# Low parts of the weights in the heads' stage: on VectorE instead of GpSimd, and two projection steps later

## The chip, the cores and the metric

The kernel runs on one core of a Trainium2 chip. The core's engines work side by side, each through its own queue of instructions in a fixed order: TensorE (PE in the profile, its weight loads PEld), VectorE (DVE), ScalarE (ACT), GpSimd (POOL) and SyncE (SP), whose queue issues most DMAs. The metric is the device time of one execution in microseconds; lower is better.

## The reference, cut to what matters

One layer of a hybrid encoder on 528 prompt positions and 128 sample positions, in fp32. One projection `w_in` feeds eight heads of gated delta rule and a state space model (S5); both go through one output projection, a layer norm and a gated feed-forward network.

```python
proj = h @ w_in                                   # (656 x 2048) @ (2048 x 5136)
qkv_pre, z, a_logit, b_logit, u = split(proj)
qkv = silu(conv4(qkv_pre)); q, k = l2_normalize(q), l2_normalize(k)
...                                               # per head, over blocks of positions:
w = w_val_c - k_cd_c @ s                          # s: the 128 x 128 state
o = q_dec_c @ s + qk_c @ w
s = s * g_tot_c + k_dec_c.T @ w
...
o = o * rsqrt(mean(o * o) + eps) * dn_norm_w * silu(z)
y5 = s5_ssm(u); y5 = gelu(y5); y5 = y5 * sigmoid(y5 @ s5_w_glu + s5_b_glu)
x1 = layer_norm(alpha * h + concat(o, y5) @ w_out)
y = layer_norm(alpha * x1 + (silu(x1 @ w_gate) * (x1 @ w_up)) @ w_down)
```

## The kernel before

A product of fp32 matrices is made of three products in the faster fp32r format. Each operand is split in a high part and a low part, and a tile of output sums high × high, low × high and high × low. The activations are split once (`hh`, `hl`); the weights are split as they come in, in units of 128 × 1024.

The life of one weight unit goes through four places. `push` notes a load, a DMA into a tile `raw` of which there are two. `halves` makes `whi` (a copy to fp32r on ScalarE, L160) and the low part `wlo` (`raw` minus `whi`, L161); there are three buffers of each. `advance` calls both ahead of need, and `unit` hands the oldest unit out. `project` uses it: a projection has two units, each of two halves of eight steps of three matmuls, `pj<-hh,whi`, `pj<-hl,whi` and `pj<-hh,wlo` (L498 to L500). When the second half of a unit begins, `project` calls `advance(2)`, which makes the parts of the unit two further on; so a weight made in one unit is used one whole unit later.

The engine of the low parts comes from `self.lows`, an endless list. It holds VectorE in the S5 stage and from the GLU on; `heads_phase` sets it to GpSimd (L700).

The heads' stage runs from 340 to 935 us. `heads_phase` gives `drive` a row of generators (`fill`: the projections of q, k, v of six heads, of z of eight, then the GLU) and a list of jobs with step numbers. A projection yields after every six matmuls; such a stretch is a projection step, and after each one `drive` advances the jobs that are due. Head h begins 47 steps after head h − 1, with three jobs: `delta_prep` (transposes, the decay `dt`, the blocks `gt` and `qk`, the prepared rows `vc` of L847, the inverse of a triangular block by `inv16`, and an inverse root in steps named `nrm`), `delta_double` (the inverse, doubled up) and `delta_scan` (the chain over the blocks). In the scan each block goes TensorE (`ps_seq<-st,kq`, L992, L993), VectorE (`rhs`, L995, and the sum `vc` of L978), TensorE (L1001), ScalarE (`x`), TensorE (L1006), VectorE (the new state `st`, L1011), and again; the sample positions go beside it (`srhs` L1034, `xm` L1045, `sb` L1047 and L1056). At its end come an inverse root (steps named `rms`), the scaled rows `vc` (L956) and their transposes on TensorE (L393).

A context `behind` adds an order that no data asks for: an instruction in it comes after a given one, on whatever engine. `drive` puts each job's step behind the last matmul so far, and `project` puts the parts of a unit there. A scheduler makes each engine's order from the program, the dependencies and these orders.

GpSimd does in this stage, per head, the scaling of `gt` (L857, three instructions), of `sb` (L1047), the masked block `gm` (L889), a few small copies, and the low parts.

Of the kernel before, what the change touches and what calls it, by code (L numbers as in the profile page):

```python
# [11 lines left out]
F32 = mybir.dt.float32  # L12
# [82 lines left out]
class Builder:  # L95
    def __init__(self, tc, io, stop=None):
        self.tc, self.nc, self.io, self.stop = tc, tc.nc, io, stop
        self.booted = None
        self.lows = cycle([self.nc.vector])
        self.units = []  # L100
        self.loaded = []
        self.issued = []
        self.quads = []
        self.raws = []
        self.later = deque()
# [45 lines left out]
    def halves(self, val, n):  # L151
        nc = self.nc
        w = val.shape[1]
        hi = self.wp.tile([P, 1024], F32R, name="whi", tag="whi", bufs=3)[:, :w]
        lo = self.wp.tile([P, 1024], F32R, name="wlo", tag="wlo", bufs=3)[:, :w]
        if self.booted is None:
            nc.vector.tensor_copy(hi, val)
            nc.gpsimd.tensor_sub(lo, val, hi.bitcast(F32))
        else:
            nc.scalar.activation(hi, val, AF.Copy)  # L160
            next(self.lows).tensor_sub(lo, val, hi.bitcast(F32))  # L161
        return hi.rearrange("p (k n) -> p k n", n=n), lo.rearrange("p (k n) -> p k n", n=n)

    def advance(self, ahead):

        while self.units and len(self.issued) < ahead:
            if not self.loaded:
                self.loaded.append(self.units[0][0]())
            self.issued.append(self.units.pop(0)[1](self.loaded.pop(0)))
        if self.units and not self.loaded:  # L170
            self.loaded.append(self.units[0][0]())

    def unit(self, ahead=2):
        self.advance(1 + ahead)
        return self.issued.pop(0)


# [185 lines left out]
    def drive(self, fill, jobs):  # L363


        jobs = [[x, n, lo, hi, 0] for x, n, lo, hi in jobs]

        def advance(at):
            for job in jobs:
                x, n, lo, hi, _ = job  # L370
                while job[4] <= n and job[4] * (hi - lo) < n * (at - lo):
                    job[4] += 1
                    with self.behind(self.last.ins):
                        if next(x, self) is self:
                            job[4] = n + 1
            if self.later:
                with self.behind(self.last.ins):
                    if next(self.later[0], self) is self:
                        self.later.popleft()

        at = 0
        for at, _ in enumerate(chain(*fill), 1):
            advance(at)
        while self.later or any(job[4] <= job[1] for job in jobs):
            at += 1
            advance(at)
# [307 lines left out]
    def heads_phase(self):  # L694
        self.head = {}

        self.gm16, self.pp16 = (self.dl.tile([96, 5, 96], F32, name=x) for x in ("gm16", "pp16"))
        for x in (self.gm16, self.pp16):
            self.nc.gpsimd.memset(x, 0.0)
        self.lows = cycle([self.nc.gpsimd])  # L700
        self.left = 2 * (3 * (H - PRE) + H)
        fill = [self.qkv(h) for h in range(PRE, H)] + [self.project_z(i) for i in range(H)]
        fill += [self.glu_start()] + [self.glu(m) for m in range(8)]
        jobs = []
        for h in range(H):
            at = PERIOD * h
            jobs.append((self.delta_prep(h), 23, at, at + 23))
            jobs.append((self.delta_double(h), 8, at + 30, at + 54))
            jobs.append((self.delta_scan(h), 35, at + 54, at + 2 * PERIOD + 2))
        jobs.append((self.gelu(), 8, 290, 390))  # L710
        jobs.append((self.glu_load(), 1, 396, 397))
        jobs.append((self.glu_split(), 4, 408, 422))
        self.drive(fill, jobs)
        self.nc.sync.dma_start(self.io["o_conv"], self.co)

    def qkv(self, h):
# [832 lines left out]
    def w_out(self):  # L1549
        tc, nc, io = self.tc, self.nc, self.io  # L1550
        v, a, g = nc.vector, nc.scalar, nc.gpsimd
        with tc.tile_pool(name="acc", bufs=1, side="right", reuse_waits="tile") as ap:
# [83 lines left out]
            def step(nm, i):  # L1636
                x, y = halves(i)
                if nm == "T1":
                    o = x[:, 0:8]
                    v.tensor_sub(o, y[:, 0:8], o)  # L1640
                elif nm == "T2":
                    o = x[:, 0:8]
                    v.tensor_sub(o, y[:, 8:16], o)
                elif nm == "T3":
                    o = y[:, 0:8]
                    g.tensor_sub(o, y[:, 8:16], o)
                elif nm == "B22":
                    o = y[:, 8:16]
                elif nm == "T4":
                    o = x[:, 8:16]  # L1650
                    g.tensor_sub(o, o, x[:, 0:8])
                    nc.sync.dma_start(self.scr_f.rearrange("k p n -> p k n")[:, :, 64 * i : 64 * i + 64], o)
                    return
                put(nm, o, 64 * i, 64)
# [399 lines left out]
```

## Time and profile before

| | |
|---|---|
| time, median of 3 runs | 2956.07 us (2953.01 to 2960.33) |
| the profiled execution | 2958.67 us, its span 2956.8 us |
| TensorE busy over the span | 2817.0 us, 95% |
| VectorE, ScalarE, GpSimd busy | 2248.6, 1174.9, 469.4 us (76, 40, 16%) |
| the chain that ended last, by engine | TensorE 71%, VectorE 15%, DMA 4%, issue 3%, ScalarE 2%, GpSimd 1% |
| mean granted TensorE clock over the span | 0.985 of full speed |

The span is what the trace covers; the time is a little longer. The shares are means over stages, so the heads' stage is read by itself, in a window. Of an engine's wait the profile names the instruction whose end released it. The durations in the timelines are from start to end of an instruction: one that stands still while it runs shows as a long one.

### The profile page before, as it was taken

The numbers are of one execution on the slowest core, as the hardware profiler recorded it, in microseconds if no ns is written. First come the engines' busy times: TensorE is split into PE (matmuls) and PEld (weight loads), VectorE is DVE, ScalarE is ACT, GpSimd is POOL, SyncE is SP. The second block draws the span as 40 slices with busy tenths as digits, with TensorE's granted clock in tenths as the row PEclk, the third lists the DMA queues.
The fourth block names the chain that finished last, engine by engine and source line by source line (L and its number), as shares of the span: only waits on it lengthen the run. The fifth ranks groups of instructions, "written<-read, shape, count | busy, mean of one in ns | idle before, by whom it ended". The sixth has DMA issues, their size and how long they took to land.

```text
span 2956.8 us, 47411 instructions
## 1 busy us (share of the span) xinstructions
PE 2817.0 (95%) x18707; PEld 2694.2 (91%) x18707; DVE 2248.6 (76%) x3715; ACT 1174.9 (40%) x2141; POOL 469.4 (16%) x371
## 2 busy tenths in 40 slices
PE   6999999999899999889999999999999999999996
PEld 5999988888889878689999999999999999999995
DVE  9899776666655744897878787878888667778788
ACT  3555334444434513643434343434343343323234
POOL 3122333233221300430000000000000021111114
PEclk9999999999999999999999999999999999999998
DMA  4333333433446634553434443444444645553553
GB/s 157 102 107 102 109 95 89 98 88 89 126 126 207 218 102 131 152 155 117 148 117 148 117 149 117 148 117 144 122 148 119 238 139 202 203 183 111 188 179 128
DMA packets 477983, 409.14 MB, mean 138 GB/s; under 512 B 50708, under 2 KB 424644, under 8 KB 473392
## 3 DMA queue, kind: packets, MB, share of 16 engines
q1 hardware_dynamic: 475960, 403.01, 44.6%
q8 instruction: 147, 2.41, 0.4%
q10 hardware_dynamic: 1800, 3.11, 0.3%
q14 instruction: 76, 0.62, 0.1%
HBM read 319.80 MB, written 86.26 MB: 137 GB/s over the span
## 4 chain that ended last, share of the span: by engine, by line
PE 71%; DVE 15%; DMA 4%; issue 3%; ACT 2%; POOL 1%; SPq 0%; DVEq 0%; ACTq 0%; POOLq 0%
PE pb_m L1474 14%; PE pb_m L1476 14%; PE pb_m L1475 14%; PE pd L1476 5%; PE pd L1474 5%; PE pd L1475 5%; PE pj L498 3%; PE pj L500 3%; PE pj L499 3%; DVE wlo L161 2%; ACT whi L160 1%; DVE pr L782 1%; DMA raw<-in_w_out 1%; PE ps_prep L393 1%; DVE z L1353 1%
## 5 line engine op out<-in xcount | busy, mean ns | idle before, releaser
L160 ACT ACTIVATE whi<-raw 128x1024 fp32r<-128x1024 f32 x408 | 431.4, 1057 | 600.8 <-PE pb_m L1476 148.7
L161 DVE TENSOR_TENSOR wlo<-raw,whi 128x1024 fp32r<-128x1024 f32 x330 | 424.7, 1287 | 166.4 <-ACT whi L160 165.7
L161 POOL TENSOR_TENSOR wlo<-raw,whi 128x1024 fp32r<-128x1024 f32 x78 | 190.4, 2442 | 1624.6 <-ACT whi L160 1608.7
L498 PE MATMUL pj<-hh,whi 128*128 128x328 f32 (+1 forms) x1248 | 424.9, 340 | 0.0
L500 PE MATMUL pj<-hh,wlo 128*128 128x328 f32 (+1 forms) x1248 | 395.6, 317 | 0.0
L499 PE MATMUL pj<-hl,whi 128*128 128x328 f32 (+1 forms) x1248 | 394.9, 316 | 0.0
L160 ACT ACTIVATE whi<-rq 128x1024 fp32r<-128x1024 f32 x190 | 201.5, 1061 | 376.1 <-PE pb_m L1475 257.8
L1474 PE MATMUL pd<-hp,whi 128*128 128x320 f32 x960 | 297.9, 310 | 8.4 <-ACT whi L160 8.4
L1476 PE MATMUL pd<-hp,wlo 128*128 128x320 f32 x960 | 298.0, 311 | 1.8 <-POOL wlo L161 1.3
L1475 PE MATMUL pd<-hp,whi 128*128 128x320 f32 x960 | 297.6, 310 | 0.0
L498 PEld LDWEIGHTS pj<-hh,whi 128*128 128x128 f32 x1248 | 238.2, 191 | 17.5 <-issue 14.7
L499 PEld LDWEIGHTS pj<-hl,whi 128*128 128x128 f32 x1248 | 238.4, 191 | 1.0 <-issue 0.8
L500 PEld LDWEIGHTS pj<-hh,wlo 128*128 128x128 f32 x1248 | 237.4, 190 | 0.5 <-issue 0.2
L161 DVE TENSOR_TENSOR wlo<-rq,whi 128x1024 fp32r<-128x1024 f32 x176 | 224.2, 1274 | 15.6 <-ACT whi L160 14.6
L193 DVE TENSOR_TENSOR raw<-rq 128x1024 f32<-128x1024 f32 x128 | 158.6, 1239 | 60.7 <-DMA rq<-in_ffn_w_gate 31.2
L1800 DVE TENSOR_TENSOR s<-pb_m,s 128x320 f32<-128x320 f32 x308 | 149.8, 487 | 69.8 <-PE pb_m L1476 67.8
L1905 DVE TENSOR_TENSOR acf<-acf,pd 128x640 f32<-128x640 f32 x184 | 146.8, 816 | 70.4 <-PE pd L1476 69.6
L1474 PEld LDWEIGHTS pd<-hp,whi 128*128 128x128 f32 x960 | 181.5, 189 | 9.5 <-ACT whi L160 9.5
L1476 PEld LDWEIGHTS pd<-hp,wlo 128*128 128x128 f32 x960 | 181.6, 189 | 3.0 <-POOL wlo L161 2.0
L1475 PEld LDWEIGHTS pd<-hp,whi 128*128 128x128 f32 x960 | 181.5, 189 | 0.0
L1811 ACT ACTIVATE hh<-hq 128x560 fp32r<-128x560 f32 (+1 forms) x88 | 57.6, 654 | 158.3 <-DMA scr_h<-hh 74.7
L1475 PE MATMUL pb_m<-T2l,whi 128*128 128x320 f32 x352 | 109.5, 311 | 3.4 <-DVE T2l L1629 3.4
(585 smaller groups left out, 7657.9 us busy)
## 6 DMA issues: line engine op xcount, KB each, us to landing
rq<-in_ffn_w_gate SPq DMA_DIRECT2D x88, 512.0 KB
rq<-in_ffn_w_up SPq DMA_DIRECT2D x88, 512.0 KB
raw<-in_w_in SPq DMA_DIRECT2D x80, 512.0 KB
rq<-in_ffn_w_down SPq DMA_DIRECT2D x80, 512.0 KB
raw<-in_w_out SPq DMA_DIRECT2D x48, 512.0 KB
hp<-scr_h SPq DMA_DIRECT2D x18, 1280.0 KB
scr_h<-hh SPq DMA_DIRECT2D x80, 280.0 KB
scr_h<-hq SPq DMA_DIRECT2D x20, 1120.0 KB
```

The lines of the kernel that those rows point to most:

```text
L160: nc.scalar.activation(hi, val, AF.Copy)
L161: next(self.lows).tensor_sub(lo, val, hi.bitcast(F32))
L193: self.nc.vector.tensor_tensor(o, x, y, op=op)
L498: nc.tensor.matmul(o, whi[:, k], self.h_hi[u][:, k, s], start=(kk == 0), stop=False)
L499: nc.tensor.matmul(o, whi[:, k], self.h_lo[u][:, k, s], start=False, stop=False)
L500: self.last = nc.tensor.matmul(o, wlo[:, k], self.h_hi[u][:, k, s], start=False, stop=(kk == KT - 1))
L1474: mm(out, sh, mh, start=first, stop=False)
L1475: mm(out, sh, ml, start=False, stop=False)
L1476: self.last = mm(out, sl, mh, start=False, stop=last)
L1800: v.tensor_tensor(t, x, y, op=ALU.add)
L1811: a.activation(h, x, AF.Copy)
L1905: v.tensor_tensor(x, x, ps, op=ALU.subtract if o[0] == "-" else ALU.add)
```

## The change

`halves` no longer issues the low part in the heads' stage. It notes it in a list `due` with a count of two. After every projection step `drive` counts down and issues what has come to zero, behind the last matmul, on the engine that `self.lows` gives. `heads_phase` no longer sets that to GpSimd, so it is VectorE. `advance` and `unit` issue all that is still due. After `drive` the list is off again; the units of the GLU inside `drive` are noted in it too.

```diff
--- before.py
+++ after.py
@@ -96,6 +96,7 @@
     def __init__(self, tc, io, stop=None):
         self.tc, self.nc, self.io, self.stop = tc, tc.nc, io, stop
         self.booted = None
+        self.late_lows, self.due = False, []
         self.lows = cycle([self.nc.vector])
         self.units = []
         self.loaded = []
@@ -158,11 +159,23 @@
             nc.gpsimd.tensor_sub(lo, val, hi.bitcast(F32))
         else:
             nc.scalar.activation(hi, val, AF.Copy)
+            if self.late_lows:
+                self.due.append([2, lo, val, hi])
+            else:
+                next(self.lows).tensor_sub(lo, val, hi.bitcast(F32))
+        return hi.rearrange("p (k n) -> p k n", n=n), lo.rearrange("p (k n) -> p k n", n=n)
+
+    def low_parts(self, steps=None):
+
+        for x in self.due:
+            x[0] -= 1
+        while self.due and (steps is None or self.due[0][0] <= 0):
+            _, lo, val, hi = self.due.pop(0)
             next(self.lows).tensor_sub(lo, val, hi.bitcast(F32))
-        return hi.rearrange("p (k n) -> p k n", n=n), lo.rearrange("p (k n) -> p k n", n=n)
 
     def advance(self, ahead):
 
+        self.low_parts()
         while self.units and len(self.issued) < ahead:
             if not self.loaded:
                 self.loaded.append(self.units[0][0]())
@@ -172,6 +185,7 @@
 
     def unit(self, ahead=2):
         self.advance(1 + ahead)
+        self.low_parts()
         return self.issued.pop(0)
 
 
@@ -366,6 +380,8 @@
         jobs = [[x, n, lo, hi, 0] for x, n, lo, hi in jobs]
 
         def advance(at):
+            with self.behind(self.last.ins):
+                self.low_parts(1)
             for job in jobs:
                 x, n, lo, hi, _ = job
                 while job[4] <= n and job[4] * (hi - lo) < n * (at - lo):
@@ -697,7 +713,7 @@
         self.gm16, self.pp16 = (self.dl.tile([96, 5, 96], F32, name=x) for x in ("gm16", "pp16"))
         for x in (self.gm16, self.pp16):
             self.nc.gpsimd.memset(x, 0.0)
-        self.lows = cycle([self.nc.gpsimd])
+        self.late_lows = True
         self.left = 2 * (3 * (H - PRE) + H)
         fill = [self.qkv(h) for h in range(PRE, H)] + [self.project_z(i) for i in range(H)]
         fill += [self.glu_start()] + [self.glu(m) for m in range(8)]
@@ -711,6 +727,7 @@
         jobs.append((self.glu_load(), 1, 396, 397))
         jobs.append((self.glu_split(), 4, 408, 422))
         self.drive(fill, jobs)
+        self.late_lows = False
         self.nc.sync.dma_start(self.io["o_conv"], self.co)
 
     def qkv(self, h):
```

The order on GpSimd, beside the fourth head's scan, before (names are out<-in; `co`, `xp` are the convolution's small copies):

```order
L624 COPY xp<-scT 128x8x3
L161 TENSOR_TENSOR wlo<-raw,whi 128x1024
L857 TENSOR_TENSOR gt<-gt,fc 112x3x112
L857 TENSOR_TENSOR gt<-gt,fc 96x2x96
L857 TENSOR_TENSOR gt<-gt,fc 128x128
L161 TENSOR_TENSOR wlo<-raw,whi 128x1024
L1047 TENSOR_TENSOR sb<-sb,ee 128x1024
L635 COPY co<-xp 128x3
L636 COPY co<-xp 128x24
L161 TENSOR_TENSOR wlo<-raw,whi 128x1024
L624 COPY xp<-scT 128x8x3
L889 TENSOR_TENSOR gm_4018<-gt,consts 96x15x16
```

The same place after the change (line numbers are those of the changed program, up to 17 higher):

```order
L640 COPY xp<-scT 128x8x3
L874 TENSOR_TENSOR gt<-gt,fc 112x3x112
L874 TENSOR_TENSOR gt<-gt,fc 96x2x96
L874 TENSOR_TENSOR gt<-gt,fc 128x128
L1064 TENSOR_TENSOR sb<-sb,ee 128x1024
L651 COPY co<-xp 128x3
L652 COPY co<-xp 128x24
L640 COPY xp<-scT 128x8x3
L906 TENSOR_TENSOR gm_4018<-gt,consts 96x15x16
```

The low parts are gone from GpSimd, the rest stands in the same order; all 52 of the stage are gone so.

The order on VectorE in the fourth head's scan, from a step of the inverse's copying (`pr`) to the first sums of the block, before (`nrm_*` is the inverse root of the next head):

```order
L782 TENSOR_TENSOR pr<-pr,ti 41x512
L118 TENSOR_TENSOR nrm_t<-nrm_t,ss 128x6
L1011 SCALAR_TENSOR_TENSOR st<-st,ee,ps_seq 128x128
L789 TENSOR_REDUCE ti<-pr 41x8x8
L119 SCALAR_TENSOR_TENSOR nrm_y<-nrm_t,nrm_y 128x6
L642 SCALAR_TENSOR_TENSOR yc<-xp,cwc,yc 128x680
L794 COPY ti<-ti 41x16x16
L117 SCALAR_TENSOR_TENSOR nrm_t<-nrm_y 128x6
L995 SCALAR_TENSOR_TENSOR rhs<-ps_seq,fc,vc 96x128
L118 TENSOR_TENSOR nrm_t<-nrm_t,ss 128x6
L978 TENSOR_TENSOR vc<-o_7405,ps_seq 112x128
```

And after:

```order
L799 TENSOR_TENSOR pr<-pr,ti 41x512
L119 TENSOR_TENSOR nrm_t<-nrm_t,ss 128x6
L1028 SCALAR_TENSOR_TENSOR st<-st,ee,ps_seq 128x128
L806 TENSOR_REDUCE ti<-pr 41x8x8
L120 SCALAR_TENSOR_TENSOR nrm_y<-nrm_t,nrm_y 128x6
L658 SCALAR_TENSOR_TENSOR yc<-xp,cwc,yc 128x680
L811 COPY ti<-ti 41x16x16
L118 SCALAR_TENSOR_TENSOR nrm_t<-nrm_y 128x6
L174 TENSOR_TENSOR wlo<-raw,whi 128x1024
L119 TENSOR_TENSOR nrm_t<-nrm_t,ss 128x6
L1012 SCALAR_TENSOR_TENSOR rhs<-ps_seq,fc,vc 96x128
L120 SCALAR_TENSOR_TENSOR nrm_y<-nrm_t,nrm_y 128x6
```

One low part has come in, behind the state `st` and ahead of the next `rhs`.

The order on VectorE at the end of the first head's scan, up to the start of the root `rms` (L927 waits for the doubled inverse), before:

```order
L623 MEMSET xp 128x3
L649 SCALAR_TENSOR_TENSOR kq<-kq,yc 128x528
L650 SCALAR_TENSOR_TENSOR kq<-kq,yc 128x128
L1011 SCALAR_TENSOR_TENSOR st<-st,ee,ps_seq 128x128
L978 TENSOR_TENSOR vc<-o_5225,ps_seq 96x128
L927 TENSOR_SCALAR rt<-ps_inv 32x5x32
L949 TENSOR_SCALAR ms<-ms 128x6
```

And after:

```order
L639 MEMSET xp 128x3
L174 TENSOR_TENSOR wlo<-raw,whi 128x1024
L665 SCALAR_TENSOR_TENSOR kq<-kq,yc 128x528
L916 TENSOR_TENSOR rt<-rt,ps_inv 96x5x3x16
L666 SCALAR_TENSOR_TENSOR kq<-kq,yc 128x128
L1028 SCALAR_TENSOR_TENSOR st<-st,ee,ps_seq 128x128
L995 TENSOR_TENSOR vc<-o_5225,ps_seq 96x128
L944 TENSOR_SCALAR rt<-ps_inv 32x5x32
L966 TENSOR_SCALAR ms<-ms 128x6
```

A low part has come in ahead of the last state `st` of the head, and a small instruction of the inverse (`rt`, L916) has moved in between; the root `rms` itself follows unchanged.

## Rows read from the trace of the kernel before

**Rows 1.** The page, part 1: busy us (share of the span) and instructions of each engine.

```profile
PE 2817.0 (95%) x18707; PEld 2694.2 (91%) x18707; DVE 2248.6 (76%) x3715; ACT 1174.9 (40%) x2141; POOL 469.4 (16%) x371
```

**Rows 2.** Windows, heads' stage: us, busy PE, PEld, DVE, ACT, POOL, PEclk, DMA share, GB/s.

```profile
340.00:935.00 595.00, 562.08 (x4067) 518.30 (x4067) 381.16 (x1044) 239.81 (x771) 174.56 (x150) 0.98 0.42 111
```

**Rows 3.** TensorE's waits, 340 to 935 us: us in total, times, longest.

```profile
PE ps_seq L992 <- DVE st L1011: 12.4, 6, 3.2
PE ps_seq L1040 <- issue: 4.5, 2, 3.4
PE ps_seq L393 <- DVE vc L956: 4.3, 4, 2.3
PE ps_seq L1054 <- DVE vc L978: 2.9, 3, 2.3
PE ps_prep L393 <- DVE vc L847: 1.9, 3, 1.2
PE ps_prep L832 <- DVE vc L847: 1.9, 1, 1.9
PE ps_inv L892 <- DMA tt<-scr_r: 1.9, 1, 1.9
PE ps_seq L1031 <- DMA sb<-in_state_delta: 0.8, 1, 0.8
```

**Rows 4.** Instructions of line 161, 340 to 935 us: duration ns min/median/max, first and last.

```profile
L161 POOL TENSOR_TENSOR wlo<-raw,whi x52: 2357/2390/2828, 347.8 to 926.0; 128x1024 fp32r<-128x1024 f32 x52
```

**Rows 5.** The same line, 60 to 340 us.

```profile
L161 DVE TENSOR_TENSOR wlo<-raw,whi x28: 1198/1217/1589, 69.8 to 338.9; 128x1024 fp32r<-128x1024 f32 x28
```

**Rows 6.** Timeline of three engines near 640 us (start us, us), and line 864's instructions.

```profile
635.98 2.39 POOL L161 TENSOR_TENSOR wlo<-raw,whi 128x1024 fp32r<-128x1024 f32 x1 [4.37 <-ACT whi L160]
635.96 2.42 DVE L864 TENSOR_SCALAR own<-consts,ee 128x2 f32<-128x2 f32 x1
643.51 0.46 PE L992 MATMUL ps_seq<-st,kq 128*96 128x128 f32 x2 [2.23 <-DVE st L1011]
L864 DVE TENSOR_SCALAR own<-consts,ee x8: 212/216/2423, 373.3 to 848.1; 128x2 f32<-128x2 f32 x8
```

**Rows 7.** Timeline, GpSimd and VectorE near 777 us, and a like instruction.

```profile
776.48 2.76 POOL L161 TENSOR_TENSOR wlo<-raw,whi 128x1024 fp32r<-128x1024 f32 x1 [10.84 <-ACT whi L160]
776.95 3.16 DVE L782 TENSOR_TENSOR pr<-pr,ti 41x512 f32<-41x512 f32 x1
642.13 1.00 DVE L782 TENSOR_TENSOR pr<-pr,ti 41x512 f32<-41x512 f32 x1
```

**Rows 8.** Timeline, VectorE and GpSimd near 464 us.

```profile
463.17 0.31 DVE L927 TENSOR_SCALAR rt<-ps_inv 32x160 f32<-32x160 f32 x1 [1.95 <-PE ps_inv L922]
464.62 2.42 POOL L161 TENSOR_TENSOR wlo<-raw,whi 128x1024 fp32r<-128x1024 f32 x1 [3.16 <-ACT whi L160]
464.81 2.25 DVE L118 TENSOR_TENSOR rms_t<-rms_t,ms 128x6 f32<-128x6 f32 x1
```

**Rows 9.** Timeline, VectorE: first and last of the 29 held instructions.

```profile
368.94 2.27 DVE L642 SCALAR_TENSOR_TENSOR yc<-xp,cwc,yc 128x680 f32<-128x680 f32 x1
927.06 1.99 DVE L1430 TENSOR_TENSOR hl<-ge,hh 128x640 fp32r<-128x640 f32 x1
```

**Rows 10.** Waits of SP's DMA queue, 340 to 935 us: us in total, times, longest.

```profile
SPq L146 <- POOL wlo L161: 28.1, 14, 5.5
```

**Rows 11.** Timeline, VectorE and TensorE just after rows 6.

```profile
645.17 0.33 DVE L995 SCALAR_TENSOR_TENSOR rhs<-ps_seq,fc,vc 96x128 f32<-96x128 f32 x1
646.25 0.46 PE L1001 MATMUL ps_seq<-rhs,rt 96*96 96x128 f32 x2 [0.19 <-DVE vc L978]
```

**Rows 12.** Windows of 4 us, columns as in rows 2.

```profile
782.00:786.00 4.00, 3.71 (x16) 3.71 (x17) 2.85 (x13) 1.17 (x5) 0.00 (x0) 0.57 0.46 81
```

**Rows 13.** Timeline, GpSimd and VectorE near 756 us.

```profile
755.74 1.57 POOL L857 TENSOR_TENSOR gt<-gt,fc 112x336 f32<-112x336 f32 x3 [4.94 <-DVE fc L854]
755.90 3.61 DVE L1397 TENSOR_SCALAR gt__8801<-gt__8801 128x640 f32<-128x640 f32 x1 [0.25 <-ACT gt__8801 L1396]
```

## The prediction

> **What bounds the kernel now.** First the page: TensorE is busy 95% of the span [rows 1], so the time falls only where TensorE stands still or runs slowly, or where matmuls go away; the change takes away none. Then the table by stage. The change is confined to the heads' stage, 340 to 935 us: there TensorE is busy 562 of 595 us, VectorE 381 and GpSimd 175, at a mean granted clock of 0.98 [rows 2]. So 33 us of standing still and some slow running are all that can be won here. Third, TensorE's waits in that stage by what ended them [rows 3]: 12.4 us for the state `st` of the scan, 4.3 for the normalised rows `vc` (L956), 4.5 for `srhs` (named "issue"), 2.9 for `vc` (L978), twice 1.9 for the prepared `vc` (L847), 1.9 for a DMA of the inverse. Nearly all of them end with a VectorE instruction; none ends with a low part of a weight. VectorE is 64% busy, so over the stage it isn't the bound: these waits come from single late instructions.
>
> **Why those instructions are late.** Each of the 52 low parts runs 2.39 us on GpSimd [rows 4]; 52 × 2.39 = 124 of GpSimd's 175 us. In the stage before this one the same instruction, on VectorE, takes 1.22 us [rows 5]. Now look at the two engines side by side. GpSimd starts a low part at 635.98 and takes 2.39; VectorE's `own`, two columns wide, starts at 635.96 and takes 2.42 us where its kind takes 0.21 to 0.22, ending with it; TensorE then waits 2.23 us for `st` [rows 6]. The same at 776.48: a `pr` takes 3.16 us, against 1.00 for the like one at 642.13 [rows 7], and the longest wait for `st`, 3.2 us, follows. And at 464.62: one small step of the inverse root takes 2.25 us [rows 8], and TensorE waits for the `vc` that ends the chain. I compared each VectorE instruction under a low part with the short ones of its form: 29 of the 52 cases run over 0.6 us too long, 52 us in all; the first took 2.27 us, the last 1.99 [rows 9]. The other 23 hold next to nothing, VectorE being idle or in an instruction that isn't held.
>
> The Trainium skill has the rule for it (SBUF — State Buffer, § SBUF: two separate sides): VectorE and GpSimd share a pair of ports that is an exclusive lock, held for the whole instruction, and who starts first blocks the other. Held rows that end with the low part agree with it. By the same rule a moved low part, which reads two SBUF operands, can itself be held by what stays on GpSimd; that would add an estimated 3 us of VectorE time and change the sum by less than its rounding.
>
> **The change, part by part.** *Removed:* 52 instructions on GpSimd, 124 us, and with them 52 us of held VectorE time. *Added:* 52 low parts on VectorE, 52 × 1.22 = 63 us. VectorE's net load rises by about 11 us, to 66% of the stage. *Moved:* each low part now enters two projection steps later. That is 12 matmuls; by 562 us for 4067 matmuls one takes 0.138 us [rows 2], so 1.7 us. It ends at about 1.7 − 2.39 + 1.22 = 0.5 us later than today. A weight made in one unit is used a whole unit later, 48 matmuls or 6.6 us, and no wait of today ends with a low part [rows 3], so I cost the delay at nothing; if VectorE's queue stood over 6 us behind, that cover would be gone and each case cost what exceeds it. The low part's end also frees the raw tile, and SP's queue stands still for that: 28.1 us in 14 waits, up to 5.5, and every DMA behind the waiting one with it [rows 10]. 0.5 us more in each of 14 is 7 us of SP's time; TensorE's waits that end with a DMA are the inverse's 1.9 and one of 0.8 for a state [rows 3], so at most 2 × 0.5 = 1 us of it can reach TensorE today. I take 0, and leave the 1 us to the range. The remaining units of the GLU get the two steps too; their low parts are on VectorE already.
>
> What the waits give back, one by one:
> - `st`, 12.4 us in six waits. At 643.51 the hold is 2.42 − 0.21 = 2.2 us. By the order of after, the low part now stands behind `st` and ahead of `rhs`. `rhs` ends at 645.50 and TensorE waits again at 646.25, 0.19 us [rows 11]: no slack there. So VectorE runs 2.2 us earlier up to `st`, only 2.2 − 1.2 = 1.0 earlier after it, and TensorE gains about 1.0 and not 2.2. In five of the six the low part is ahead of `st` or of the next `rhs`, in one behind both. The ends are 6 × 1.0 = 6 and the full 12.4; I take 1.4 each, 8.4, nearer to the case worked out.
> - `vc` L956, 4.3 us in four waits. Here the low part stands well ahead of the chain, before an instruction for which VectorE sat idle 1.95 us [rows 8], and the next one right behind the last `vc`. So most of it goes: 3.4; ends 1.5 (where the low part fills the place of the hold) and 4.3.
> - `vc` L978, 2.9: two waits follow a held instruction; 1.2, ends 0 and 2.9.
> - `vc` L847, 3.8 in the two rows: one of the waits, 1.9, follows a late DMA and stays; 1.0 of the rest, ends 0 and 1.9.
> - the inverse's DMA, 1.9: the chain ahead of it was held three times, and TensorE's instruction that waits moves some four projection groups later by the order; 1.0, ends 0 and 1.9.
>
> Together 8.4 + 3.4 + 1.2 + 1.0 + 1.0 = 15.0 us, ends 7.5 and 23.4.
>
> *The clock.* After the long wait at 782 the granted clock is 0.57 for 4 us [rows 12], that is mostly the lower level, 1.2 GHz; there are six such stretches, each after a wait of 1.9 us or more. A mean of 0.98 over 595 us costs about 12 us (6 to 18 by its rounding). Where the waits shrink, some of these stretches go: I take 5 us, ends 0 and 10.
>
> *Against it:* a low part that lands in front of an instruction that TensorE waits for, where today no hold was. The nearest row is the low part's own 1.22 us [rows 5]; 23 of the 52 replace a hold of nearly nothing. I take 2 us for two such places, ends 0 and 32 (below).
>
> *What stays:* GpSimd keeps `gt` (1.57 us per head) and, right behind it, `sb`; the two hold a GELU instruction on VectorE for 3.61 us, and the 3.4 us wait for `srhs` follows [rows 13], which I leave in full.
>
> Sum: 15.0 + 5 − 2 = 18 us off the profiled 2958.67, some 2941; that run lies 2.6 over the median 2956.07, so the forecast is **2938**.
>
> **Rivals.** *1. The hold is only exchanged.* In every case the 1.2 us sit in the same backlog that the 2.2 us sat in, each wait shrinks by the low end (7.5 in all), the stretches at half clock stay, and new waits cost 2: 2956.1 − 5.5 = 2950.6, no change. For it speaks the case at 643.51; against it that in the chain of `vc` VectorE has an idle 1.95 us for it. *2. VectorE becomes the bound (slower).* Low parts enter at fixed steps of the projection; where VectorE is in a backlog already, as around 636 to 643, each pushes `st`, `rhs` or `srhs` back. If half of the 52 land so, 26 × 1.22 = 32 us of new waits against 15 + 2 saved: +15, 2971. Break-even is some 14 such places (17 us). Against it: VectorE is busy 64% and ends at 66. *3. The low part is late for TensorE.* Excluded as far as the cover of 6.6 us reaches; it would show as a wait ended by `wlo`. *4. It doesn't do what it says:* the order shows all 52 off GpSimd, so no.
>
> The Trainium skill speaks in favour on another count (GPSIMD Engine Reference, § 3.1): elementwise work takes 1.96 times as long on GpSimd; the rows here, 2.39 against 1.22, agree. Nothing in the sum hangs on it.
>
> **How the numbers follow.** The forecast case 0.72, the exchange 0.20, slower 0.08. A measurement of this kernel can tell about 0.3%, 8.9 us, from no change. Faster by more than that means under 2947.2: nearly all of the first case, 0.72. Within: 0.21. Slower: 0.07. The optimistic end is 23.4 + 10 − 0 = 33 us, 2923; the range reaches up over the exchange, 2952, and leaves out the slower case and a little more.
>
> **What would show it.** Right: GpSimd's low parts gone and its busy time near 50 us in the stage; `own`, the inverse root and `pr` with no maximum above 1.5 us; the waits for `st` at half or less, with some turned into waits for `rhs`; VectorE near 392 us; fewer stretches at the lower clock. Wrong: waits for `st` unchanged in sum (rival 1), a wait ended by `wlo` (rival 3), new waits for `rhs` or `srhs` (rival 2).

## The result, and the profile after

The changed kernel takes 2921.69 us (median of 4 runs, 2920.22 to 2925.71) beside 2958.2 for the kernel before: a ratio of 0.9879, with a 95% interval of 0.9862 to 0.9896. That is some 36 us less, 1.2%. The forecast had the direction and the mechanism, and half the size: 18 us, with 2923 as the low end of the range.

First the page of the changed kernel, part 1, as in [rows 1]:

```profile
PE 2808.6 (96%) x18707; PEld 2690.1 (92%) x18707; DVE 2247.2 (77%) x3767; ACT 1171.6 (40%) x2141; POOL 347.1 (12%) x319
```

TensorE's share rises by a point; its busy time falls by 8 us, some 7 of them by the clock: the stretches at its lower level sum to 90.9 us over the run before and to 77.5 after, by the clock's record in the traces. GpSimd has lost 122 us, the 52 low parts. The heads' stage now ends some 33 us earlier, by the first matmul of the output projection, before and after:

```profile
985.57 0.40 PE L1474 MATMUL pb_m<-whi,mix0h 128*128 128x512 f32 x1
953.02 0.40 PE L1491 MATMUL pb_m<-whi,mix0h 128*128 128x512 f32 x1
```

In each run of this document the same 6451 matmuls stand ahead of it, so it serves as the mark of the stage's end, which the window puts 50 us ahead of it. Nearly the same distance holds at the last matmul (2903.3 and 2936.2), so all of the gain between the two profiled runs is made in this stage. Its window, 340 to 903 us, columns as in [rows 2] (us, busy PE, PEld, DVE, ACT, POOL, PEclk, DMA share, GB/s):

```profile
340.00:903.00 563.00, 554.18 (x4082) 514.51 (x4081) 383.24 (x1100) 238.86 (x773) 52.33 (x99) 0.99 0.44 119
```

VectorE is as busy as before in all, 383 us against 381 [rows 2], though it does 52 instructions more: what it lost in holds it spends on low parts. TensorE's waits in that window, the counterpart of [rows 3] (us in total, times, longest):

```profile
PE ps_seq L1057 <- issue: 2.7, 1, 2.7
PE ps_seq L1009 <- DVE st L1028: 1.5, 3, 0.7
PE ps_seq L1071 <- DVE vc L995: 1.0, 1, 1.0
PE ps_prep L849 <- DVE vc L864: 0.5, 1, 0.5
PE ps_seq L409 <- DVE vc L973: 0.4, 1, 0.4
PE ps_seq L1018 <- ACT o L1014: 0.2, 1, 0.2
```

The six waits for `st`, 12.4 us, are three of 1.5 us in all; the transposes of `vc` (409 here, 393 before) wait 0.4 instead of 4.3; the wait for the inverse's DMA, 1.9 us, is gone. Over all rows of that view it is 8.4 us, against 32.8 before. 24.4 of the 33 us are found in this view alone.

The next rows show that the holds by low parts are gone: the instructions of `own`, of one step of the inverse root, and the low parts themselves, in the changed kernel (duration ns min/median/max, first and last start):

```profile
L881 DVE TENSOR_SCALAR own<-consts,ee x8: 209/216/224, 371.8 to 816.5; 128x2 f32<-128x2 f32 x8
L119 DVE TENSOR_TENSOR rms_t<-rms_t,ms x24: 156/166/168, 456.3 to 902.9; 128x6 f32<-128x6 f32 x24
L174 DVE TENSOR_TENSOR wlo<-raw,whi x53: 1203/1217/2810, 349.7 to 900.2; 128x1024 fp32r<-128x1024 f32 x53
```

The maximum of `own` is 0.22 us, where it was 2.42 [rows 6]; that of the inverse root's step is 0.17, where it was 2.25 [rows 8]. The low parts take 1.22 us, as in [rows 5], with two exceptions of 2.81. This is the first, on GpSimd and VectorE, and behind it what `gt` and `sb` hold later:

```profile
482.48 1.89 POOL L1064 TENSOR_TENSOR sb<-sb,ee 128x1024 f32<-128x1024 f32 x1
482.64 2.81 DVE L174 TENSOR_TENSOR wlo<-raw,whi 128x1024 fp32r<-128x1024 f32 x1
734.63 1.86 POOL L874 TENSOR_TENSOR gt<-gt,fc 112x336 f32<-112x336 f32 x3 [11.04 <-DVE fc L871]
736.46 1.89 POOL L1064 TENSOR_TENSOR sb<-sb,ee 128x1024 f32<-128x1024 f32 x1
735.18 3.85 DVE L1415 TENSOR_TENSOR gt__8801<-gt__8801,yf 128x640 f32<-128x640 f32 x1
```

GpSimd's `sb`, which stayed there, starts 0.16 us before the low part, and the low part takes 1.6 us longer. It happens twice in the stage (482 and 546 us), 3.2 us together. This is near the 3 us that the prediction estimated by the rule of the Trainium skill (SBUF — State Buffer, § SBUF: two separate sides) that the two engines' shared ports are locked for a whole instruction. At 735 us a step of the GELU takes 3.85 us beside `gt` and `sb`, against 0.81 in the run e7 below, where it comes behind them; the wait for `srhs` follows.

Last the clock: the granted TensorE clock around the only long wait that is left, the one for `srhs` that ends at 739.78 us (window, columns as above):

```profile
739.00:743.00 4.00, 3.22 (x13) 3.25 (x14) 3.08 (x7) 2.33 (x4) 0.58 (x1) 0.50 0.23 82
747.00:751.00 4.00, 4.00 (x24) 3.05 (x23) 2.71 (x12) 1.26 (x6) 0.00 (x0) 1.00 0.03 9
```

From 739 us it is 0.50, the lower of the two levels (1.2 GHz); TensorE stood still for 2.7 us up to 739.78. Of 20.5 us at the lower level in the stage 6.8 are left, by the clock's record in the traces.

### The profile page after: what moved, and what is told of

It is laid out like the page before. It is cut to its first block, busy times and chain, and to the rows that moved or that the text cites. A ratio compares the mean times of both kernels' runs of the same rounds, so it can differ in the third digit from the quotient of the medians.

```text
span 2923.9 us, 47341 instructions
## 1 busy us (share of the span) xinstructions
PE 2808.6 (96%) x18707; PEld 2690.1 (92%) x18707; DVE 2247.2 (77%) x3767; ACT 1171.6 (40%) x2141; POOL 347.1 (12%) x319
## 4 chain that ended last, share of the span: by engine, by line
PE 75%; DVE 12%; DMA 5%; issue 3%; ACT 2%; POOL 2%; SPq 0%; DVEq 0%; ACTq 0%; POOLq 0%
PE pb_m L1493 14%; PE pb_m L1491 14%; PE pb_m L1492 14%; PE pd L1493 5%; PE pd L1491 5%; PE pd L1492 5%; PE pj L514 5%; PE pj L516 4%; PE pj L515 4%; DVE wlo L165 2%; DMA raw<-in_w_out 1%; ACT whi L161 1%; DMA raw<-in_w_in 1%; PE ps_prep L409 1%; DVE acc L1588 1%
## 5 line engine op out<-in xcount | busy, mean ns | idle before, releaser
L165 DVE TENSOR_TENSOR wlo<-raw,whi 128x1024 fp32r<-128x1024 f32 x322 | 414.8, 1288 | 165.2 <-ACT whi L161 164.1
L165 POOL TENSOR_TENSOR wlo<-raw,whi 128x1024 fp32r<-128x1024 f32 x26 | 63.4, 2439 | 1381.4 <-ACT whi L161 1381.4
L207 DVE TENSOR_TENSOR raw<-rq 128x1024 f32<-128x1024 f32 x128 | 156.6, 1223 | 60.8 <-DMA rq<-in_ffn_w_gate 31.9
L1491 PE MATMUL pb_m<-T1h,whi 128*128 128x320 f32 x352 | 110.0, 312 | 2.6 <-ACT T1h L1645 2.6
```

The source lines that it names most:

```text
L207: self.nc.vector.tensor_tensor(o, x, y, op=op)
L1491: mm(out, sh, mh, start=first, stop=False)
```

## The experiments

All times are medians; the ratio is against runs of the kernel before on the same chip. "Waits" is the sum of TensorE's waits in the heads' stage, over all rows of that view, as above; the window ends near the same place of each run.

| kernel | low parts made by | us | ratio (95%) | waits, us |
|---|---|---|---|---|
| before | GpSimd | 2955 to 2958 | 1 | 32.8 |
| the change | VectorE, two steps late | 2921.69 | 0.9879 (0.9862 to 0.9896) | 8.4 |
| e2 | GpSimd, two steps late | 2958.52 | 1.0002 (0.9988 to 1.0017) | 31.1 |
| e1 | VectorE, at once | 2923.28 | 0.9883 (0.9853 to 0.9914) | 9.8 |
| e3 | both engines | 2999.24 | 1.0135 (1.0103 to 1.0167) | 49.3 |
| e7 | GpSimd, 16 of 1024 columns | 2917.60 | 0.9873 (0.9858 to 0.9887) | 8.6 |
| e6 | VectorE, twice | 2927.22 | 0.9911 (0.9894 to 0.9928) | 14.7 |
| e5 | GpSimd; gt, sb, gm on VectorE | 2963.61 | 1.0032 (1.0017 to 1.0047) | 37.0 |
| e4 | VectorE; gt, sb, gm too | 2922.02 | 0.9881 (0.9854 to 0.9908) | 6.8 |
| e8 | VectorE, and a GpSimd memset | 2929.27 | 0.9910 (0.9895 to 0.9925) | 12.6 |

Three theories stood against each other. A: the gain comes from GpSimd's low parts no longer holding VectorE instructions. B: it comes from the delay, which keeps a low part from standing ahead of what TensorE waits for. C: it comes from the new order of the instructions.

**The move without the delay (e1).** In the changed kernel:

```diff
-        self.late_lows = True
```

> The low parts on VectorE, but entered at once with their high parts: the move without the delay. Theory A (the gain comes from GpSimd's low parts no longer holding VectorE instructions): the holds are gone here too, so nearly all of the gain stays; 2921 to 2928 us beside 2921.7 for the change. Theory B (the delay is what keeps the low parts from standing ahead of what TensorE waits for): a low part of 1.2 us stands ahead of the state or the next right side more often, half of the gain is lost; 2935 to 2945 us.

Measured: 2923.28 us, a ratio of 0.9883 beside 0.9879. TensorE's waits, first rows:

```profile
PE ps_seq L1056 <- issue: 5.6, 2, 3.1
PE ps_seq L1070 <- DVE vc L994: 1.1, 1, 1.1
PE ps_seq L1008 <- DVE st L1027: 0.7, 2, 0.5
```

The wait for `st` is as small as in the change (0.7 us here, 1.5 there). The delay gives nothing that can be measured; B falls.

**The delay without the move (e2).** In the changed kernel:

```diff
         self.late_lows = True
+        self.lows = cycle([self.nc.gpsimd])
```

> The delay without the move: GpSimd still makes the low parts, two projection steps later. Theory A: the holds are as many, only 1.7 us later; 2950 to 2962 us, no change against the kernel before, and TensorE's waits in the heads' stage sum to 27 to 38 us (32.8 before, 8.4 after the change). Theory B: a third of the gain or more; 2930 to 2946 us.

Measured: 2958.52 us, no change against the kernel before. TensorE's waits:

```profile
PE ps_seq L1010 <- DVE st L1029: 12.3, 6, 3.2
PE ps_seq L409 <- DVE vc L974: 4.3, 4, 2.3
PE ps_inv L910 <- DMA tt<-scr_r: 1.8, 1, 1.8
```

They are those of [rows 3], nearly to the tenth: 12.3 us for `st`, 4.3 for `vc` L974 (L956 before), 1.8 for the inverse. So the move is the whole gain.

**Both engines (e3).** The changed kernel with the old holds added to it:

```diff
                 self.due.append([2, lo, val, hi])
+                nc.gpsimd.tensor_sub(lo, val, hi.bitcast(F32))
```

> The change as it is, and beside it GpSimd makes each low part too, at the old place, into the same buffer; VectorE makes it again two steps later. So the order of the changed kernel, with the holds of the old one. Theory A: the holds take 52 us of VectorE again on top of the 63 us of low parts; the gain is lost and some more: 2950 to 2980 us, and the small VectorE instructions have maxima of 2.4 us again. Theory C (the gain comes from the new order of the instructions, above all more projection matmuls between the state's product and the next one): the gain stays, 2920 to 2930 us.

Measured: 2999.24 us, 42 us over the kernel before on that chip, 19 us beyond the upper end of what A gave. The window of the stage, two of TensorE's waits, and one of VectorE's:

```profile
340.00:980.00 640.00, 590.50 (x4139) 542.10 (x4138) 439.81 (x1110) 244.38 (x784) 192.53 (x153) 0.96 0.41 108
PE ps_seq L1010 <- DVE st L1029: 16.6, 10, 3.1
PE ps_seq L410 <- DVE vc L974: 8.2, 6, 2.5
DVE wlo L175 <- POOL wlo L164: 45.4, 21, 4.2
```

By the starts in the traces the order differs from the changed kernel's in some 16 rows of 18,707 on TensorE and some 90 of 3,767 on VectorE. With the holds back the waits for `st` are ten and 16.6 us, and the mean clock is 0.96. The new order alone doesn't keep the gain, then: nearly the same order is 78 us slower once GpSimd runs its low parts again. But the run is no clean sum of holds and low parts. Both low parts write the same tile, so VectorE's has to come after GpSimd's, and VectorE stood idle for 45.4 us, in 21 cases, until GpSimd's had ended. How much of the loss beyond A's range is this wait, and how much the low parts on top of the holds, is not told apart; nor does the run finish C by itself.

**Neither holds nor low parts (e7).** The kernel before, in its own order on TensorE and on VectorE, with GpSimd's low part cut to 16 columns; the third product takes the high part in the low part's place:

```diff
-            next(self.lows).tensor_sub(lo, val, hi.bitcast(F32))
+            nc.gpsimd.tensor_sub(lo[:, :16], val[:, :16], hi[:, :16].bitcast(F32))
+            lo = hi
```

> The kernel before, in its own order on TensorE and VectorE, with GpSimd's low part cut to 16 of 1024 columns and the third product reading the high part in its place: no holds, no work added on VectorE, no delay. Theory A1: the holds are the whole loss and VectorE's low parts cost nothing, so it takes as long as the change: 2916 to 2926 us. Theory X: without the 9 us or so that the low parts cost on VectorE it is faster than the change: 2905 to 2914 us. Theory C (part of the gain is the new order on TensorE): 2930 to 2945 us.

Measured: 2917.60 us, a ratio of 0.9873. The window and two of the waits:

```profile
340.00:903.00 563.00, 554.09 (x4105) 514.85 (x4104) 329.01 (x1057) 241.65 (x775) 63.11 (x151) 1.00 0.46 121
PE ps_seq L1046 <- issue: 4.0, 2, 2.9
PE ps_seq L998 <- DVE st L1017: 1.0, 1, 1.0
```

VectorE is 329 us busy here, 52 us less than in the kernel before [rows 2] with the same instructions: as much as the prediction had counted in held time. It is 54 us less than in the change, and yet TensorE waits 8.6 us, where it waits 8.4 in the change. The holds are the whole loss of the kernel before (0.9873, some 38 us). The low parts on VectorE, in the order that the scheduler makes for them, cost 2 to 4 us of the whole by the ratios and the medians, an amount that the two intervals don't tell from none. It is the outcome of A1, and it finishes C: the old order, without the holds, has the whole gain.

**Low parts twice (e6).** The changed kernel:

```diff
-            next(self.lows).tensor_sub(lo, val, hi.bitcast(F32))
+            eng = next(self.lows)
+            for _ in range(2):
+                eng.tensor_sub(lo, val, hi.bitcast(F32))
```

> The change, with each late low part made twice on VectorE, one after the other: another 60 x 1.2 = 73 us on VectorE and no holds. Theory A1 (a low part on VectorE costs TensorE next to nothing, the scheduler puts it and TensorE's order where there is room): 2921 to 2928 us. Theory X (as the prediction priced it, a low part in front of a state or a right side costs TensorE 1.0 to 1.2 us in the place, some 9 us in all per 52): 2930 to 2945 us.

Measured: 2927.22 us, 0.9911, some 5.5 us over the change for another 73 us of VectorE work. The window, the two largest groups of the waits for `zs`, that for `st`, and the first matmul of the output projection:

```profile
340.00:913.00 573.00, 557.77 (x4070) 514.71 (x4069) 439.89 (x1150) 239.17 (x772) 59.53 (x99) 0.99 0.44 118
PE pj L516 <- DVE zs L1087: 3.5, 2, 2.6
PE pj L1493 <- DVE zs L1087: 2.8, 1, 2.8
PE ps_seq L1011 <- DVE st L1030: 0.7, 1, 0.7
963.22 0.40 PE L1493 MATMUL pb_m<-whi,mix0h 128*128 128x512 f32 x1
```

VectorE is 440 us busy, 77% of the stage, and TensorE waits 0.7 us for `st`. But the output projection begins at 963.2 us here, 10 us later than in the change; the stage's waits sum to 14.7, 6.3 of them for `zs`, a step of the gate from z. In the output projection behind it TensorE waits 6.3 us in the change, 5.2 of them for low parts of that stage, and shows no wait here, which gives part of the 10 us back. So the second low parts cost 10 us in the stage and 5.5 in the whole: by the time it is A1's outcome, by the stage it is near what X charges (9 us per 52). It is little beside the holds, which put that mark 36 us later (985.6 us before, 949.2 in e7): 2.4 us of VectorE work at a place, longer than the hold that it replaces, hardly lets TensorE wait for `st`. The order shows one reason. Between the product with the state and the next product with the right side, in the third block of heads 3 to 7, where five of the six waits for `st` were, TensorE has 12, 11, 17, 5 and 12 projection matmuls in the kernel before, 15, 19, 25, 8 and 14 in the changed one, and 28, 19, 44, 29 and 36 in this one. The chain gets more room in the order as VectorE's part in it grows; holds give it none, for e3, with GpSimd's low parts added, has the changed kernel's numbers. It is not the whole reason: in the second head the number falls, 12, 6 and 5, and in e1 it is 9 in three of the heads, without new waits. That the room makes the low parts cheap was not isolated; no run had them on VectorE in the old order of TensorE.

**The rest of GpSimd's work instead (e5).** The kernel before, with three edits of this kind (`gt`, `sb`, `gm`):

```diff
-        g.tensor_tensor(sb, sb, self.gtots[:, h, :, None].to_broadcast([P, 8, P]), op=ALU.mult)
+        v.tensor_tensor(sb, sb, self.gtots[:, h, :, None].to_broadcast([P, 8, P]), op=ALU.mult)
```

> The kernel before, with its low parts on GpSimd, but the scaling of gt and of sb and the masked block gm on VectorE: the other GpSimd work moved instead. Theory A (it is the low parts' 124 us that hold VectorE, in 29 of 52 cases): most of the loss stays; only the wait for srhs, 4.5 us, and a little of the clock go: 2943 to 2955 us. Rival (it is GpSimd's own queue, gt and sb standing behind low parts, that delays the chain): a good half of the gain is had, 2930 to 2940 us.

Measured: 2963.61 us, 0.3% slower than the kernel before: a miss of A's figure too, which had a small gain. TensorE's waits:

```profile
PE ps_seq L992 <- DVE st L1011: 14.7, 8, 2.8
PE ps_inv L892 <- DMA tt<-scr_r: 2.3, 1, 2.3
```

The waits for `st` rise from 12.4 to 14.7 us. The long wait for `srhs`, 3.4 us, is 0.5 here, but others for it come, 4.0 in all against 4.5. `gt` and `sb` stand behind no low part here, and nothing is won. In the kernel before VectorE waits only 1.0 us for GpSimd in the stage, TensorE shows no wait for it, and SP's waits for `gt` are the same before and after the change (109 and 108 us), so that rival falls. That more VectorE work costs where the holds are still there would fit this run; it isn't isolated.

**The rest of GpSimd's work too (e4).** The same three edits in the changed kernel.

> The change, and what is left on GpSimd per head of the three larger operations (scaling of gt, of sb, the masked block gm) on VectorE as well. Theory A: 28 us of GpSimd work stop holding VectorE, at the price of some 20 us more on VectorE; the last long wait, 2.7 us for srhs with the lower clock behind it, goes: 2914 to 2921 us. Rival (VectorE's added work lands ahead of what TensorE waits for): 2922 to 2932 us.

Measured: 2922.02 us, the same as the change, 1 us above A's range and at the lower end of the rival's. Three of TensorE's waits:

```profile
PE ps_seq L409 <- DVE vc L973: 2.2, 3, 1.6
PE ps_prep L849 <- DVE qk L855: 2.2, 1, 2.2
PE ps_seq L1057 <- issue: 0.2, 1, 0.2
```

The wait for `srhs` (L1057) fell from 2.7 to 0.2 us, as A had it; others came, 2.2 for `qk` and 2.2 for `vc`, and took it back.

**A memset in the place of the low part (e8).** The changed kernel, in its order on TensorE and VectorE, with an operation of GpSimd that only writes:

```diff
                 self.due.append([2, lo, val, hi])
+                nc.gpsimd.memset(lo.bitcast(F32), 0.0)
```

> The change, with a memset of the low part's tile by GpSimd at the old place: an operation of the same output that reads nothing, in exactly the changed kernel's order on TensorE and VectorE. If only a GpSimd operation that reads holds VectorE: 2920 to 2927 us, and maxima of the small VectorE instructions under 0.6 us. If any GpSimd operation on the tile memory holds it: 2935 to 2985 us, by how long the memset takes.

Measured: 2929.27 us, some 7.5 over the change, between the two ranges. First the memsets as a group, then two of them and the VectorE instructions beside them:

```profile
L164 POOL MEMSET wlo<- 128x1024 f32 x53 | 50.5, 953 | 165.9 <-PE pj L517 148.9 <-DVE rms_t L119 8.4 <-DVE rms_t L118 8.4
639.17 0.95 POOL L164 MEMSET wlo<- 128x1024 f32 x1
639.00 1.49 DVE L656 TENSOR_SCALAR yc<-xp,cwc 128x680 f32<-128x680 f32 x1 [0.92 <-ACT xp L646]
649.87 0.95 POOL L164 MEMSET wlo<- 128x1024 f32 x1 [4.62 <-PE pj L517]
650.08 0.17 DVE L118 SCALAR_TENSOR_TENSOR rms_t<-rms_y 128x6 f32<-128x6 f32 x1
650.28 0.17 DVE L119 TENSOR_TENSOR rms_t<-rms_t,ms 128x6 f32<-128x6 f32 x1
```

A memset takes 0.95 us. `yc<-xp,cwc`, a TENSOR_SCALAR that reads one tile and a column of factors, starts 0.17 us before one and takes 1.49 us, against 0.57 in the kernel before at 631.6 us and in the changed one at 615.1. The steps of the inverse root, which read two tiles or one tile twice, run in their usual 0.17 us right under the other. Over the stage the VectorE instructions that a memset stretched by 0.5 us or more were TENSOR_SCALARs, and the few queued right behind one.

**GpSimd's low parts elsewhere (e9, e10, e11).** The changed kernel with VectorE alone in the last products of the feed-forward network (e9: `cycle([v, v, v, nc.gpsimd])` becomes `cycle([v])`), and in its first units (e10: `cycle([g, v])` becomes `cycle([v])`), and the changed kernel again.

> The change, and in the last products of the feed-forward network (2311 to 2900 us), where every fourth low part is GpSimd's, all low parts on VectorE too. GpSimd's low parts hold a VectorE instruction for 1.3 to 2.1 us in 13 cases there, but TensorE waits only 1.7 us for a low part of GpSimd in the stage. If holds cost what they cost in the heads' stage (0.5 to 0.7 us of time per us held): 2908 to 2914 us. If they lie off the path here: 2919 to 2926 us.

> The change, and in the first units of the feed-forward network (near 1200 us), where every second low part is GpSimd's until the next stage, all low parts on VectorE too. Few low parts are concerned, and GpSimd's other work there stays and holds VectorE as before: 2918 to 2926 us, no change against the change. If the holds of those few decide: 2910 to 2917 us.

> The changed kernel again, beside the two others on one chip: 2919 to 2925 us, 0.987 to 0.989 of the kernel before.

Measured: e9 2919.05 us (0.9870, 0.9852 to 0.9889), e10 2928.09 (0.9905, 0.9882 to 0.9929), and the change 2921.42 (0.9880, 0.9858 to 0.9902). e9 is not told apart from the change; e10 is 7 us slower, in a stretch (1150 to 1260 us) in which VectorE is 95 of 110 us busy in the change. Neither is clearly faster than the change.

## Why the prediction was right in direction and wrong in size

The reason for the late instructions, GpSimd's low parts holding VectorE, is shown by e2 and e7. What failed is the sum, 18 us. The two profiled runs lie 33 us apart, and 31 of these are found: 24.4 us of waits and 6.8 of the clock. The step that failed is the price of the waits: those for `st` were to shrink by the hold less the low part's own 1.22 us, with the slack of the old order, and of the others those without a held instruction right ahead were to stay. Of the 13 us that were missing 6.9 lie in the five waits that the sum lists, 2.5 in `srhs` and small ones, 2.0 in the price set against the gain, and 1.8 in the clock.

- *`st`.* Forecast 8.4 us of 12.4; 10.9 came. The step was "1.0 earlier after it", from a `rhs` without slack in the order before [rows 11]. Here is that place in the changed kernel, VectorE and TensorE:

```profile
624.87 0.33 DVE L1028 SCALAR_TENSOR_TENSOR st<-st,ee,ps_seq 128x128 f32<-128x128 f32 x1
626.91 1.21 DVE L174 TENSOR_TENSOR wlo<-raw,whi 128x1024 fp32r<-128x1024 f32 x1
628.15 0.33 DVE L1012 SCALAR_TENSOR_TENSOR rhs<-ps_seq,fc,vc 96x128 f32<-96x128 f32 x1
625.25 0.46 PE L1009 MATMUL ps_seq<-st,kq 128*96 128x128 f32 x2 [0.41 <-DVE st L1028]
629.14 0.46 PE L1018 MATMUL ps_seq<-rhs,rt 96*96 96x128 f32 x2
```

  The low part does stand between `st` and `rhs`, but TensorE reaches the product with `rhs` 3.9 us after that with the state, where it was 2.7 us [rows 6, 11], with 19 projection matmuls between them instead of 11. I took the slack from the order of before, though the order of after lay open and had other numbers of matmuls. The wait at the first product is 0.41 us and the second shows none, against 2.23 and 0.19; I had 1.0 us of gain and 2.0 came.
- *`vc` L956.* Forecast 3.4, and 3.9 came.
- *`vc` L847, `vc` L978 and the inverse's DMA.* Forecast 1.0, 1.2 and 1.0; it was 3.3, 1.9 and 1.9. The wait of 1.9 us behind a late DMA that "stays" did not: it is 0.5 in the change and 0.3 in e7, and 1.6 and 1.8 in e2 and e5, where GpSimd makes the low parts. So it was theirs as well. The traces show the way, here before (two rows) and after (two rows); `cd` is an input of the head that is stored, and the load of `gb` is queued on SP behind that store:

```profile
348.20 2.54 DVE L649 SCALAR_TENSOR_TENSOR cd<-cd,yc 128x528 f32<-128x528 f32 x1 [0.51 <-ACT cd L646]
352.38 0.42 SPq L825 DMA_DIRECT2D gb<-scr_c  x1
348.88 0.71 DVE L665 SCALAR_TENSOR_TENSOR cd<-cd,yc 128x528 f32<-128x528 f32 x1 [0.52 <-ACT cd L662]
351.24 0.42 SPq L842 DMA_DIRECT2D gb<-scr_c  x1
```

  `cd` runs beside a low part (from 347.77 us) before, and the load leaves 1.1 us later. In the same way two steps of the inverse are held, 2.48 us at 382.76 and 2.44 at 389.24, and the store of `ti` leaves at 395.57, against 389.99 in the change, each time right behind VectorE's last step. So it was the holds, through DMAs that wait for VectorE. SP's own waits for low parts [rows 10] did not shrink: 31.9 us in 14 waits in the change.
- *`srhs`.* Left in full, 4.5; 2.7 is left in the change, 4.0 in e7 and 0.2 in e4. That `gt` and `sb` make the long one agrees with the row at 735 us above and with e4.
- *All waits.* I took back 15.0 us in five terms, with 23.4 as the upper end; these five gave 21.9, and all rows 24.4. e7 gives the figure that was to be forecast: without holds 8.6 us of waits are left.
- *The clock.* Forecast 5 us. The stretches at half the clock went from 20.5 to 6.8 us; half of the difference is 6.8 us. Right within its ends of 0 and 10. (The record has five stretches before, one of them twice as long as the others, where I counted six; the mean of 0.98 gives 9 to 15 us by its rounding, not 6 to 18, and half of 20.5 is 10.)
- *Against it, 2 us.* No new wait of note came: the product with `rhs` waits 0.2 us in the change (L1018), against 0.7 before (L1001), and the one new row of some size is 0.5 behind `so`. By the times, 2 to 4 us over e7, a price of 2 isn't excluded. Rival 1, the exchange, falls: the waits shrank by 24.4 us and not by 7.5. So does rival 2; in e6 twice the work makes the stage 10 us longer, not 32.
- *The delay at nothing.* Right: e1 and the change don't differ, and no wait ends with a low part in the stage.
- *GpSimd near 50 us, VectorE near 392.* 52 and 383; the second is 9 us under.

## What to carry to other kernels

Time in which an instruction stands still beside another engine's instruction cost more here than the same time of planned work: 52 us of holds on an engine that was 64% busy cost 38 us, while 73 us of added work on the same engine cost 10 us in the stage and 5.5 in the whole. So when a wait is traced to such holds, count all waits of the stage that vary with them, those behind a DMA that waits for a held instruction too, and not only those with a held instruction right ahead, and take the slack behind a moved instruction from the order after the change. To find what is left without the holds, shrink the holding instruction and keep the order, as in e7.

## What was not expected of the hardware

- A GpSimd memset of 0.95 us, which reads nothing, stretches a VectorE TENSOR_SCALAR with one tile operand from 0.57 to 1.49 us, and leaves instructions with two tile operands at 0.17 us; a GpSimd subtraction that reads two tiles holds both kinds (2.42 and 2.25 us, [rows 6, 8]). This agrees with the Trainium skill (SBUF — State Buffer, § Who interferes with whom), which has it that a VectorE instruction with two inputs from the tile memory contends only with a GpSimd instruction that reads there, and one in a two-port mode with either; which mode `yc` ran in the traces don't show.
- The prediction has it that who starts first blocks the other. By the recorded starts (the profile's page calls GpSimd's times rough), `sb` agrees, 0.16 us ahead of the low part that it holds; `own` doesn't, 0.02 us ahead of the low part that holds it [rows 6], nor does `yc`, 0.17 us ahead of the memset.
- Holds alone cost 38 us (the kernel before against e7), the low parts alone 2 to 4, the low parts twice 10 (e6 against e7), and holds with low parts 82 (e3 against e7). Part of the 82 is the clock, 55 us at the lower level in the stage in e3, against 20 in the kernel before and none in e7, and part may be the wait for the common tile; so that holds and added work cost more together than their sum is not shown.
